# Two head slots per attention step, their products alternating between halves of the TensorE array

## The chip, the cores and the metric

The kernel runs on one core of one Trainium2 chip. The metric is device time in microseconds of one execution. Engines are named as the profile names them: PE is TensorE (its matmuls), PEld the weight loads of TensorE, DVE is VectorE, ACT is ScalarE, POOL is GpSimd, SP is SyncE, which issues the DMAs.

## The reference

Two layers, each a mixer of three branches and a SwiGLU feed-forward, over 256 positions of width 2048, in float32. The change touches the third branch, attention with 12 heads of 64 channels in 3 groups of 4 with (window, dilation) of (128, 1), (512, 4) and (2048, 16):

```python
scores = jnp.einsum("bhrnqd,bhrnkd->bhrnqk", qb, kb) * (HEAD_DIM ** -0.5)
dist = (dilation * np.abs(rel)).astype(np.float32)
bias = -slopes[:, None, None] * dist[None]
scores = jnp.where(valid, scores + bias[:, None, None], NEG)
lse = jax.nn.logsumexp(scores, axis=-1)
p = jnp.exp(scores - lse[..., None])
out = jnp.einsum("bhrnqk,bhrnkd->bhrnqd", p.astype(v.dtype), vb)
...
w = jax.nn.softmax(jnp.stack(lses, axis=0), axis=0)
o = jnp.sum(w[..., None] * jnp.stack(outs, axis=0), axis=0)
```

The three groups of one head slot (slot s has the heads s, 4+s and 8+s) are so combined that one softmax over the keys of all three groups gives the slot's output.

## The kernel before

All weights stream from HBM, 512 KB at a time. ACT copies each piece to a rounded form (`wh`), DVE subtracts to get the rest (`wl`), and PE multiplies both with the activations, which are kept with channels in the partitions. One step of such a product is a 512-column matmul with `wh` and a 256-column matmul with `wl`; a piece of 1024 columns has eight steps. `piece()` asks for loads and splits some pieces ahead.

Work that is not a weight product is put into the queue `beside`, as pairs of a function and a cost. `product` calls `some(0.9)` after each piece, which pops entries until their costs add up to 0.9; `drain()` pops all that is left, and is called before the first `branch`. So the attention's parts are written between pieces of the products that run meanwhile: the gates in layer 0, the short convolution's `zb` and the gates in layer 1. A scheduler then sets each engine's final order. On PE it can move an instruction ahead into a place where it reckons PE would wait.

Attention works on units (s, b): slot s of 4, and half b of the positions as queries. The positions are kept in such an order that the keys of groups 1 and 2 lie in the same half as the query. So a unit's score tile has 512 columns: 256 keys of group 0, 128 of group 1, 128 of group 2. There are 8 units in each layer. A unit has four parts:

- `att_scores` (L518): three float32 products into a PSUM tile `sc`; the 64 channels of a head are the upper or the lower 64 partitions (`po`) of the `q` and `kk` tiles. Then on DVE the bias (L531, three instructions), the maximum (L533) and its negative (L534).
- `att_soft`: exponential with its sum on ACT (L538), reciprocal and scaling on DVE (L539, L540).
- `att_turn`: four 128x128 transposes on PE (L545), one copy on ACT (L547).
- `att_out`: four float32 products with `v` (L554) into 64 of the partitions of a PSUM tile `o`, then a rounded copy on ACT (L559) and the rest on DVE (L560), into `csp`, which the branch products `yc` read.

`sc`, `pt` and `o` take turns in the three PSUM buffers of `aux`. The parts of one unit are popped 1 or 2 rounds apart (`lag`):

```python
units = [(s, b, {}) for s in range(HPG) for b in range(2)]
steps = [(att_out, 4, 0.4), (att_turn, 3, 0.0), (att_soft, 1, 0.6), (att_scores, 0, 1.5)]
```

Of the kernel before, what the change touches and what calls it, by code (L numbers as in the profile page):

```python
# [9 lines left out]
F32 = mybir.dt.float32  # L10
F32R = mybir.dt.float32r
I32 = mybir.dt.int32
AF = mybir.ActivationFunctionType
OP = mybir.AluOpType
AX = mybir.AxisListType

P = 128
S = 256
# [8 lines left out]
DH = 64  # L27
NG = 3
HPG = NH // NG
# [7 lines left out]
SLOPES = [2.0 ** (-8.0 * i / NH) for i in range(1, NH + 1)]  # L37
# [12 lines left out]
def trunk(ctx, tc, xt, win, wv, wy, wo, wgu, wd, cst, fin, dist, out):  # L50
    nc = tc.nc
# [5 lines left out]
    rp = ctx.enter_context(tc.tile_pool(name="rp", bufs=2))  # L57
# [7 lines left out]
    def tile2(name):  # L65
        return t2.tile([P, 2 * S], F32, tag="t2", name=name)

    def tile2r(name):
        return t2.tile([P, 2 * S], F32R, tag="t2", name=name)
# [20 lines left out]
    def acc(name):  # L90
        return pa.tile([P, 2 * S], F32, tag="acc", name=name)

    def aux(name):
        return px.tile([P, 512], F32, tag="aux", name=name)
# [4 lines left out]
    for l in range(DEPTH):  # L99
# [8 lines left out]
        for j in range(KD):  # L108
            for i in range(NGATE):
                n = N_ZA + N_QK + N_ZB + j * NGATE + i  # L110
# [47 lines left out]
    beside = deque()  # L158
# [22 lines left out]
    def product(dst, xs, whole=False, budget=0.9):  # L181


        k = 0
        while k < len(xs):
            wh, wl, nk = piece()
            for i in range(nk):
                c = slice(i * P, (i + 1) * P)
                x = xs[k]
                last = k == len(xs) - 1  # L190
                if whole:
                    nc.tensor.matmul(dst[:, :S], wh[:, c], turned(x[:, :S]), start=k == 0, stop=False)
                    nc.tensor.matmul(dst[:, :S], wh[:, c], turned(x[:, S:]), start=False, stop=False)
                else:
                    nc.tensor.matmul(dst, wh[:, c], turned(x), start=k == 0, stop=False)  # L195
                nc.tensor.matmul(dst[:, :S], wl[:, c], turned(x[:, :S]), start=False, stop=last)  # L196
                k += 1
            some(budget)
        return dst
# [57 lines left out]
    ident = cp.tile([P, P], F32, name="ident")  # L257
# [136 lines left out]
    for l in range(DEPTH):  # L394
# [14 lines left out]
        for i in range(2 * NCT):  # L409
            if l == 0 and i < 2:  # L410
# [5 lines left out]
                ps = two[i]  # L416
            else:
                ps = product(acc("za"), norm.operand(i))
# [62 lines left out]
        q, kk = [], []  # L481
# [7 lines left out]
        for i in range(N_QK):  # L489
            dst = kk if i >= N_QK // 2 else q  # L490
            n = 2 * NCT + i
            ps = product(acc("qk"), norm.operand(n))
# [4 lines left out]
        for g in range(NG):  # L497
            pv = [acc("v")[:, :S] for _ in range(2)]
            k = 0
            while k < KD:  # L500
                wh, wl, nk = piece()
                for i in range(nk // 2):
                    w = slice(i * S, (i + 1) * S)
                    for b in range(2):
                        hi = h[k][:, b * P:(b + 1) * P]
                        lo = h[k][:, S + b * P:S + (b + 1) * P]
# [7 lines left out]
                nc.scalar.copy(v[g][b], pv[b])  # L514


        csp = [None] * 2

        def att_scores(s, b, st):
            ps = aux("sc")  # L520
            sc = st["sc"] = tile2("sc")
            po = (s % 2) * DH
            for g in range(NG):
                t = (g * HPG + s) // 2
                a, n = (0, S) if g == 0 else (S + (g - 1) * P, P)
                keys = slice(0, S) if g == 0 else slice(b * P, (b + 1) * P)
                nc.tensor.matmul(ps[:, a:a + n], q[t][po:po + DH, b * P:(b + 1) * P], kk[t][po:po + DH, keys], start=True, stop=True)
            for g in range(NG):
                a, n = (0, S) if g == 0 else (S + (g - 1) * P, P)
                d = dsb[:, b * S:(b + 1) * S] if g == 0 else dsb[:, 2 * S + (g - 1) * P:2 * S + g * P]  # L530
                nc.vector.scalar_tensor_tensor(sc[:, a:a + n], d, SLOPES[g * HPG + s], ps[:, a:a + n], op0=OP.mult, op1=OP.add)  # L531
            m = st["m"] = rp.tile([P, 4], F32, tag="m", bufs=3, name="m")
            nc.vector.reduce_max(m[:, 0:1], sc, axis=AX.X)  # L533
            nc.vector.tensor_scalar_mul(m[:, 1:2], m[:, 0:1], -1.0)  # L534

        def att_soft(s, b, st):
            sc, m = st["sc"], st["m"]
            nc.scalar.activation(sc, sc, AF.Exp, bias=m[:, 1:2], accum_out=m[:, 2:3])  # L538
            nc.vector.reciprocal(m[:, 3:4], m[:, 2:3])  # L539
            nc.vector.tensor_scalar_mul(sc, sc, m[:, 3:4])  # L540

        def att_turn(s, b, st):
            pt_ps = aux("pt")
            for i in range(4):
                nc.tensor.transpose(pt_ps[:, i * P:(i + 1) * P], st["sc"][:, i * P:(i + 1) * P], ident)  # L545
            st["pt"] = tile2("pt")
            nc.scalar.copy(st["pt"], pt_ps)  # L547

        def att_out(s, b, st):
            po = (s % 2) * DH  # L550
            o = aux("o")[po:po + DH, :P]
            vs = [v[0][0], v[0][1], v[1][b], v[2][b]]
            for i in range(4):
                nc.tensor.matmul(o, vs[i][:, s * DH:(s + 1) * DH], st["pt"][:, i * P:(i + 1) * P], start=i == 0, stop=i == 3)  # L554
            if csp[s // 2] is None:
                csp[s // 2] = tile2r("csp")
            hi = csp[s // 2][po:po + DH, b * P:(b + 1) * P]
            lo = csp[s // 2][po:po + DH, S + b * P:S + (b + 1) * P]
            nc.scalar.copy(hi, o)  # L559
            nc.vector.tensor_sub(lo, o, hi.bitcast(F32))  # L560

        units = [(s, b, {}) for s in range(HPG) for b in range(2)]
        steps = [(att_out, 4, 0.4), (att_turn, 3, 0.0), (att_soft, 1, 0.6), (att_scores, 0, 1.5)]
        for n in range(len(units) + 4):
            for f, lag, cost in steps:
                u = n - lag
                if 0 <= u < len(units):
                    beside.append((lambda f=f, u=units[u]: f(*u), cost))
            beside.append((rest, 0.9))


        bsp = [None] * NCT
# [14 lines left out]
        gates, m = {}, []  # L587
# [34 lines left out]
        for j in range(KD):  # L622
            gs = []
            for i in range(NGATE):
                whole = j == KD - 1
                ps = product(acc("gate"), h, whole)
# [6 lines left out]
                n = BRANCHES.get(j * NGATE + i)  # L633
# [7 lines left out]
        for k in range(KD):  # L641
            ps = product(acc("wo"), m)
# [7 lines left out]
        for s in range(NSEG):  # L650
            f, gu = [], []
# [14 lines left out]
            for n in range(2 * FPS):  # L666
                ps = product(acc("fgu"), norm.operand(s * 2 * FPS + n), n == 2 * FPS - 1)
# [5 lines left out]
            for k in range(KD):  # L673
                whole = last and s == NSEG - 1 and k >= KD - 2
                ps = product(acc("fd"), f, whole)
# [109 lines left out]
```

## Time and profile before

| what | value |
|---|---|
| median of 3 runs | 2645.53 us (2645.19 to 2647.09) |
| the profiled execution | 2646.27 us, span 2644.5 us |
| PE busy | 2627.1 us, 99% of the span |
| DVE busy | 1901.2 us, 72% |
| ACT busy | 1455.4 us, 55% |
| DMA | 519.36 MB, mean 196 GB/s |
| granted clock over the span | 0.998 |

PE is busy nearly all the time, DVE and ACT have room, the weights arrive at less than the rate that the start of the trace shows. Matmuls are pipelined: the duration of one overlaps the next, so what a matmul costs is read from the distance of starts, not from its duration.

### The profile page before, as it was taken

The numbers are of one execution on the slowest core, as the hardware profiler recorded it, in microseconds if no ns is written. First come the engines' busy times: TensorE is split into PE (matmuls) and PEld (weight loads), VectorE is DVE, ScalarE is ACT, GpSimd is POOL, SyncE is SP. The second block draws the span as 40 slices with busy tenths as digits, with TensorE's granted clock in tenths as the row PEclk, the third lists the DMA queues.
The fourth block names the chain that finished last, engine by engine and source line by source line (L and its number), as shares of the span: only waits on it lengthen the run. The fifth ranks groups of instructions, "written<-read, shape, count | busy, mean of one in ns | idle before, by whom it ended". The sixth has DMA issues, their size and how long they took to land.

```text
span 2644.5 us, 42907 instructions
## 1 busy us (share of the span) xinstructions
PE 2627.1 (99%) x16744; PEld 2424.0 (92%) x16744; DVE 1901.2 (72%) x2924; ACT 1455.4 (55%) x2078; POOL 128.9 (5%) x93
## 2 busy tenths in 40 slices
PE   9999999999999999999999999999999999999998
PEld 8998899999999999999999989999999999999997
DVE  7997566678876666666899965666787666666665
ACT  6548655556645545445664575555565454454555
POOL 2000000011000000000102300000200000000002
PEclk9999999999999999999999999999999999999999
DMA  6665466666666656656566545665666566666664
GB/s 220 200 203 176 156 195 207 196 203 199 199 202 200 203 200 200 203 201 202 193 202 201 188 157 181 199 207 194 204 196 211 192 201 202 201 201 201 200 205 153
DMA packets 136749, 519.36 MB, mean 196 GB/s; under 512 B 15312, under 2 KB 17248, under 8 KB 136544
## 3 DMA queue, kind: packets, MB, share of 16 engines
q1 hardware_dynamic: 135648, 515.28, 59.3%
q8 instruction: 131, 2.15, 0.3%
q10 hardware_dynamic: 864, 1.31, 0.1%
q14 instruction: 74, 0.61, 0.1%
q0 software_dynamic: 32, 0.01, 0.0%
HBM read 514.45 MB, written 2.10 MB: 195 GB/s over the span
## 4 chain that ended last, share of the span: by engine, by line
PE 98%; DMA 0%; ACT 0%; issue 0%; POOL 0%; DVE 0%; SPq 0%; POOLq 0%; ACTq 0%
PE fgu L195 22%; PE gate L195 12%; PE fgu L196 12%; PE fd L195 11%; PE gate L196 6%; PE fd L196 6%; PE wo L195 4%; PE zb L195 3%; PE qk L195 3%; PE wo L196 2%; PE za L195 2%; PE zb L196 2%; PE qk L196 2%; PE yab L605 1%; PE yab L606 1%; PE yab L604 1%
## 5 line engine op out<-in xcount | busy, mean ns | idle before, releaser
L151 DVE TENSOR_TENSOR wl<-raw,wh 128x1024 fp32r<-128x1024 f32 (+3 forms) x1086 | 1217.0, 1121 | 616.3 <-ACT wh L150 606.2
L150 ACT CAST wh<-raw 128x1024 fp32r<-128x1024 f32 (+3 forms) x1086 | 1042.3, 961 | 1083.0 <-PE fgu L195 296.7
L195 PE MATMUL fgu<-xs,wh 128*128 128x512 f32 x2688 | 881.1, 382 | 0.0
L196 PE MATMUL fgu<-xs,wl 128*128 128x256 f32 x2816 | 768.2, 273 | 0.0
L195 PEld LDWEIGHTS fgu<-xs,wh 128*128 128x128 f32 x2688 | 508.0, 189 | 70.6
L196 PEld LDWEIGHTS fgu<-xs,wl 128*128 128x128 f32 x2816 | 540.7, 192 | 0.0
L195 PE MATMUL gate<-xs,wh 128*128 128x512 f32 x1440 | 477.2, 384 | 0.0
L195 PE MATMUL fd<-fs,wh 128*128 128x512 f32 x1386 | 454.4, 382 | 0.0
L196 PE MATMUL gate<-xs,wl 128*128 128x256 f32 x1536 | 419.3, 273 | 0.0
L196 PE MATMUL fd<-fs,wl 128*128 128x256 f32 x1408 | 383.8, 273 | 0.0
L195 PEld LDWEIGHTS gate<-xs,wh 128*128 128x128 f32 x1440 | 272.2, 189 | 38.0
L195 PEld LDWEIGHTS fd<-fs,wh 128*128 128x128 f32 x1386 | 262.0, 189 | 36.4
L196 PEld LDWEIGHTS gate<-xs,wl 128*128 128x128 f32 x1536 | 294.9, 192 | 0.3 <-issue 0.3
L196 PEld LDWEIGHTS fd<-fs,wl 128*128 128x128 f32 x1408 | 270.3, 192 | 0.0
L298 POOL TENSOR_TENSOR sq<-sq 128x256 f32<-128x256 f32 x59 | 63.7, 1079 | 2189.8 <-ACT sq L293 2189.8
L195 PE MATMUL wo<-mj,wh 128*128 128x512 f32 x512 | 167.6, 382 | 0.0
L196 PE MATMUL wo<-mj,wl 128*128 128x256 f32 x512 | 138.9, 273 | 0.0
L195 PE MATMUL zb<-xs,wh 128*128 128x512 f32 x384 | 127.0, 384 | 0.0
L195 PE MATMUL qk<-xs,wh 128*128 128x512 f32 x384 | 126.0, 382 | 0.2 <-ACT wh L150 0.2
L195 PEld LDWEIGHTS wo<-mj,wh 128*128 128x128 f32 x512 | 96.5, 189 | 13.3
L196 PE MATMUL zb<-xs,wl 128*128 128x256 f32 x384 | 105.0, 274 | 0.0
L196 PE MATMUL qk<-xs,wl 128*128 128x256 f32 x384 | 104.4, 273 | 0.0
(174 smaller groups left out, 3055.4 us busy)
## 6 DMA issues: line engine op xcount, KB each, us to landing
raw<-in_wgu SPq DMA_DIRECT2D x352, 512.0 KB, 4.2
raw<-in_win SPq DMA_DIRECT2D x318, 512.0 KB, 3.6
raw<-in_wd SPq DMA_DIRECT2D x128, 704.0 KB, 4.0
raw<-in_wo SPq DMA_DIRECT2D x64, 512.0 KB, 4.2
raw<-in_wy SPq DMA_DIRECT2D x32, 640.0 KB, 4.6
raw<-in_wv SPq DMA_DIRECT2D x24, 512.0 KB, 3.9
x<-in_xt SPq DMA_DIRECT2D x7, 256.0 KB, 6.8
out_y<-x ACTq DMA_DIRECT2D x4, 256.0 KB, 3.3
```

The costliest lines, as they stand in the source:

```text
L150: nc.scalar.copy(wh[:, :b - a], raws[ci][:, a:b])
L151: nc.vector.tensor_sub(wl[:, :b - a], raws[ci][:, a:b], wh[:, :b - a].bitcast(F32))
L195: nc.tensor.matmul(dst, wh[:, c], turned(x), start=k == 0, stop=False)
L196: nc.tensor.matmul(dst[:, :S], wl[:, c], turned(x[:, :S]), start=False, stop=last)
L298: nc.gpsimd.tensor_add(self.sums[0], self.sums[0], sq)
L604: nc.tensor.matmul(dsts[k], wh[:, w], turned(ys[k][:, :S]), start=k in first, stop=False)
L605: nc.tensor.matmul(dsts[k], wh[:, w], turned(ys[k][:, S:]), start=False, stop=False)
L606: nc.tensor.matmul(dsts[k], wl[:, w], turned(ys[k][:, :S]), start=False, stop=k in final)
```

## The change

The unit becomes (t, b): a pair of slots 2t and 2t+1, which lie in the upper and the lower 64 partitions of the same `q` and `kk` tiles. There are 4 such units in a layer in place of 8. The products of the two slots are written in turn: scores alternate between the upper and the lower 64 rows of the array (into two PSUM tiles), outputs between its two halves of 64 columns (into the two halves of one PSUM tile). The negated maximum, the reciprocal and the copies to `csp` are done once for both slots. The entries of `beside` all have cost 1, so one part is popped after each piece.

```diff
-        def att_scores(s, b, st):
-            ps = aux("sc")
-            sc = st["sc"] = tile2("sc")
-            po = (s % 2) * DH
+        def att_scores(t, b, st):
+            st["ps"] = [aux("sc") for _ in range(2)]
+            st["sc"] = [tile2("sc") for _ in range(2)]
+            st["m"] = rp.tile([P, 8], F32, tag="m", bufs=3, name="m")
             for g in range(NG):
-                t = (g * HPG + s) // 2
                 a, n = (0, S) if g == 0 else (S + (g - 1) * P, P)
                 keys = slice(0, S) if g == 0 else slice(b * P, (b + 1) * P)
-                nc.tensor.matmul(ps[:, a:a + n], q[t][po:po + DH, b * P:(b + 1) * P], kk[t][po:po + DH, keys], start=True, stop=True)
+                for i, ps in enumerate(st["ps"]):
+                    po = slice(i * DH, (i + 1) * DH)
+                    nc.tensor.matmul(ps[:, a:a + n], q[g * 2 + t][po, b * P:(b + 1) * P], kk[g * 2 + t][po, keys], start=True, stop=True)
+
+        def att_far(t, b, st, i):
+            sc, ps = st["sc"][i], st["ps"][i]
             for g in range(NG):
...
+            nc.vector.reduce_max(st["m"][:, i:i + 1], sc, axis=AX.X)
+
+        def att_soft(t, b, st):
+            m = st["m"]
+            nc.vector.tensor_scalar_mul(m[:, 2:4], m[:, 0:2], -1.0)
+            for i, sc in enumerate(st["sc"]):
+                nc.scalar.activation(sc, sc, AF.Exp, bias=m[:, 2 + i:3 + i], accum_out=m[:, 4 + i:5 + i])
+
+        def att_share(t, b, st):
+            m = st["m"]
+            nc.vector.reciprocal(m[:, 6:8], m[:, 4:6])
+            for i, sc in enumerate(st["sc"]):
+                nc.vector.tensor_scalar_mul(sc, sc, m[:, 6 + i:7 + i])
...
+        def att_out(t, b, st):
+            o = aux("o")[:, :P]
             vs = [v[0][0], v[0][1], v[1][b], v[2][b]]
             for i in range(4):
-                nc.tensor.matmul(o, vs[i][:, s * DH:(s + 1) * DH], st["pt"][:, i * P:(i + 1) * P], start=i == 0, stop=i == 3)
...
+                for n in range(2):
+                    s = 2 * t + n
+                    nc.tensor.matmul(o[n * DH:(n + 1) * DH], vs[i][:, s * DH:(s + 1) * DH], st["pt"][n][:, i * P:(i + 1) * P],
+                                     start=i == 0, stop=i == 3)
...
-        units = [(s, b, {}) for s in range(HPG) for b in range(2)]
-        steps = [(att_out, 4, 0.4), (att_turn, 3, 0.0), (att_soft, 1, 0.6), (att_scores, 0, 1.5)]
-        for n in range(len(units) + 4):
+        units = [(t, b, {}) for t in range(2) for b in range(2)]
+        steps = [(att_out, 2, ()), (att_turn, 1, (0,)), (att_scores, 0, ()), (att_turn, 1, (1,)), (att_far, 0, (0,)), (att_far, 0, (1,)),
+                 (att_soft, 0, ()), (att_share, 0, ())]
+        for n in range(len(units) + 2):
```

On PE, the first scores of layer 0, before (one slot, upper half of the rows; `gate` are the gate products that run meanwhile, `qk` the q and k tiles):

```order
L196 MATMUL gate_2530<-xs_983,wl_2534 128x256
L527 MATMUL sc_2587<-qk_1106,qk_746 128x256
L527 MATMUL sc_2587<-qk_1220,qk_868 128x128
L527 MATMUL sc_2587<-qk_1334,qk_990 128x128
L195 MATMUL gate_2603<-xs_528,wh_2567 128x512
```

The same place after (`sc_2587` is written from the upper 64 rows, `sc_2588` from the lower):

```order
L196 MATMUL gate_2530<-xs_983,wl_2534 128x256
L531 MATMUL sc_2587<-qk_1106,qk_746 128x256
L531 MATMUL sc_2588<-qk_1106,qk_746 128x256
L531 MATMUL sc_2587<-qk_1220,qk_868 128x128
L531 MATMUL sc_2588<-qk_1220,qk_868 128x128
L531 MATMUL sc_2587<-qk_1334,qk_990 128x128
L531 MATMUL sc_2588<-qk_1334,qk_990 128x128
L195 MATMUL gate_2603<-xs_528,wh_2567 128x512
```

Two bursts of three products, 32 rows of gate products apart, have become one burst of six. All 16 bursts of the two layers become 8 in this way, none is cut.

On PE, the first output products of a unit in layer 0, before:

```order
L196 MATMUL gate_2802<-xs_983,wl_2806 128x256
L554 MATMUL o_2847<-pt_2781,v_1527 64x128
L554 MATMUL o_2847<-pt_2781,v_1529 64x128
L554 MATMUL o_2847<-pt_2781,v_1667 64x128
L554 MATMUL o_2847<-pt_2781,v_1805 64x128
L545 MATMUL pt_2855<-ident_132,sc_2652 128x128 x4
```

After (`pt_2767` is the first slot's turned tile, `pt_2835` the second's; at the first "..." stand 48 rows of gate products, at the second 15):

```order
L567 MATMUL o_3001<-pt_2767,v_1527 64x128
L567 MATMUL o_3001<-pt_2835,v_1527 64x128
L567 MATMUL o_3001<-pt_2767,v_1529 64x128
...
L567 MATMUL o_3001<-pt_2835,v_1529 64x128
...
L567 MATMUL o_3001<-pt_2767,v_1667 64x128
L567 MATMUL o_3001<-pt_2835,v_1667 64x128
L567 MATMUL o_3001<-pt_2767,v_1805 64x128
L567 MATMUL o_3001<-pt_2835,v_1805 64x128
```

The scheduler has put some of the eight products into earlier places. Over both layers the eight units have their outputs in pieces of 3+1+4 (three units), 3+5 (two), 8 (one) and 1+7 (two): 18 bursts in place of 16.

On PE, the end of the last unit in layer 0, after (`yc` are branch products; before, the last output products stood 49 rows of gate products ahead of the first branch product; at the "..." stand 17 rows of gate products, 4 of them, the other six outputs and 12 rows of gates, and 10 rows of gates):

```order
L619 MATMUL yc_3495<-csp_3010,wh_3496 128x256
L556 MATMUL pt_3469<-ident_132,sc_3350 128x128 x4
L556 MATMUL pt_3476<-ident_132,sc_3351 128x128 x4
L620 MATMUL yc_3495<-csp_3010,wl_3497 128x256
...
L567 MATMUL o_3483<-pt_3474,v_1527 64x128
...
L567 MATMUL o_3483<-pt_3481,v_1527 64x128
...
L618 MATMUL yc_3495<-csp_3466,wh_3496 128x256
...
L619 MATMUL yc_3495<-csp_3466,wh_3496 128x256
```

The last unit's transposes and outputs now stand inside the first branch's products. Outside the attention's stretches no engine's order changes.

## Rows read from the trace of the kernel before

**Rows 1.** The page's chain of waits, shares of the span by engine.

```profile
PE 98%; DMA 0%; ACT 0%; issue 0%; POOL 0%; DVE 0%; SPq 0%; POOLq 0%; ACTq 0%
```

**Rows 2.** Windows: stretch, its length, busy of PE, PEld, DVE, ACT, POOL.

```profile
221.00:288.00 67.00, 67.00 (x408) 58.49 (x407) 46.29 (x92) 55.84 (x81) 0.00 (x0) 1.00 0.47 157
1513.00:1606.00 93.00, 93.00 (x573) 81.42 (x573) 60.86 (x117) 67.12 (x102) 0.00 (x0) 1.00 0.46 154
```

**Rows 3.** Groups by line and shape, whole run: count, busy us, mean ns.

```profile
L554 PE MATMUL o<-pt,v 128*64 128x128 f32 x128 | 17.4, 279 | 0.0
L527 PE MATMUL sc<-qk 64*128 64x256 f32 x32 | 11.1, 428 | 0.0
L545 PE MATMUL pt<-ident,sc 128*128 128x128 f32 x64 | 10.4, 285 | 0.0
L527 PE MATMUL sc<-qk 64*128 64x128 f32 x64 | 9.7, 271 | 0.0
```

**Rows 4.** PE timeline, first scores: start, length, count in a narrow window.

```profile
221.10 0.27 PE L196 MATMUL gate<-xs,wl 128*128 128x256 f32 x1
221.43 0.27 PE L196 MATMUL gate<-xs,wl 128*128 128x256 f32 x1
221.63 0.48 PE L527 MATMUL sc<-qk 64*128 64x256 f32 x1
221.96 0.60 PE L527 MATMUL sc<-qk 64*128 64x256 f32 x3
222.17 0.49 PE L527 MATMUL sc<-qk 64*128 64x128 f32 x3
222.71 0.48 PE L195 MATMUL gate<-xs,wh 128*128 128x512 f32 x1
223.03 0.27 PE L196 MATMUL gate<-xs,wl 128*128 128x256 f32 x1
```

**Rows 5.** PEld timeline, loads of those scores and of the first outputs.

```profile
221.63 0.18 PEld L527 LDWEIGHTS sc<-qk 64*128 64x128 f32 x1 [0.23 <-issue]
221.74 0.40 PEld L527 LDWEIGHTS sc<-qk 64*128 64x128 f32 x2
...
248.09 0.85 PEld L554 LDWEIGHTS o<-pt,v 128*64 128x64 f32 x8 [0.23 <-issue]
```

**Rows 6.** PE timeline, the first outputs and the transposes behind them.

```profile
247.89 0.27 PE L196 MATMUL gate<-xs,wl 128*128 128x256 f32 x1
248.09 1.09 PE L554 MATMUL o<-pt,v 128*64 128x128 f32 x8
249.11 0.66 PE L545 MATMUL pt<-ident,sc 128*128 128x128 f32 x4
249.52 0.46 PE L195 MATMUL gate<-xs,wh 128*128 128x512 f32 x1
249.82 0.27 PE L196 MATMUL gate<-xs,wl 128*128 128x256 f32 x1
```

**Rows 7.** DVE and ACT in layer 0: a timeline row, then groups by shape.

```profile
223.92 0.79 DVE L531 SCALAR_TENSOR_TENSOR sc<-dsb,sc 128x256 f32<-128x256 f32 x3
...
L151 DVE TENSOR_TENSOR wl<-raw,wh 128x1024 fp32r<-128x1024 f32 x19 | 23.2, 1221 | 6.5 <-ACT wh L150 6.5
L533 DVE TENSOR_REDUCE m<-sc 128x1 f32<-128x512 f32 x7 | 4.7, 678 | 0.1
L540 DVE TENSOR_SCALAR sc<-sc,m 128x512 f32<-128x512 f32 x7 | 3.4, 487 | 0.2
...
L150 ACT CAST wh<-raw 128x1024 fp32r<-128x1024 f32 x18 | 18.6, 1036 | 5.0 <-issue 4.9
L538 ACT ACT_TABLE_LOAD x7 | 9.0, 1283 | 0.1
L538 ACT ACTIVATE sc<-sc,m 128x512 f32<-128x512 f32 x7 | 5.1, 722 | 0.1
L547 ACT COPY pt<-pt 128x512 f32<-128x512 f32 x4 | 2.3, 584 | 0.0
```

More of the change, by code (lines that the diff above doesn't have):

```diff
@@ L530, in att_scores @@
                 d = dsb[:, b * S:(b + 1) * S] if g == 0 else dsb[:, 2 * S + (g - 1) * P:2 * S + g * P]
[L531 to L540, printed above, removed]
@@ L542, in att_turn @@
-        def att_turn(s, b, st):
+                nc.vector.scalar_tensor_tensor(sc[:, a:a + n], d, SLOPES[g * HPG + 2 * t + i], ps[:, a:a + n], op0=OP.mult, op1=OP.add)
+            nc.vector.reduce_max(st["m"][:, i:i + 1], sc, axis=AX.X)
[4 more added lines that the diff above has]
+                nc.scalar.activation(sc, sc, AF.Exp, bias=m[:, 2 + i:3 + i], accum_out=m[:, 4 + i:5 + i])
@@ L543, in att_turn @@
+        def att_share(t, b, st):
[3 more added lines that the diff above has]
+                nc.vector.tensor_scalar_mul(sc, sc, m[:, 6 + i:7 + i])
+        def att_turn(t, b, st, n):
             pt_ps = aux("pt")
             for i in range(4):
-                nc.tensor.transpose(pt_ps[:, i * P:(i + 1) * P], st["sc"][:, i * P:(i + 1) * P], ident)
-            st["pt"] = tile2("pt")
-            nc.scalar.copy(st["pt"], pt_ps)
@@ L549, in att_out @@
-        def att_out(s, b, st):
-            po = (s % 2) * DH
-            o = aux("o")[po:po + DH, :P]
+                nc.tensor.transpose(pt_ps[:, i * P:(i + 1) * P], st["sc"][n][:, i * P:(i + 1) * P], ident)
+            pt = tile2("pt")
+            st.setdefault("pt", []).append(pt)
+            nc.scalar.copy(pt, pt_ps)
+        def att_out(t, b, st):
+            o = aux("o")[:, :P]
             vs = [v[0][0], v[0][1], v[1][b], v[2][b]]
             for i in range(4):
-                nc.tensor.matmul(o, vs[i][:, s * DH:(s + 1) * DH], st["pt"][:, i * P:(i + 1) * P], start=i == 0, stop=i == 3)
[L555 to L558, printed above, removed]
+                for n in range(2):
+                    s = 2 * t + n
+                    nc.tensor.matmul(o[n * DH:(n + 1) * DH], vs[i][:, s * DH:(s + 1) * DH], st["pt"][n][:, i * P:(i + 1) * P],
+                                     start=i == 0, stop=i == 3)
+            if csp[t] is None:
+                csp[t] = tile2r("csp")
+            hi = csp[t][:, b * P:(b + 1) * P]
+            lo = csp[t][:, S + b * P:S + (b + 1) * P]
@@ L559, in att_out @@
             nc.scalar.copy(hi, o)
             nc.vector.tensor_sub(lo, o, hi.bitcast(F32))
-        units = [(s, b, {}) for s in range(HPG) for b in range(2)]
-        steps = [(att_out, 4, 0.4), (att_turn, 3, 0.0), (att_soft, 1, 0.6), (att_scores, 0, 1.5)]
-        for n in range(len(units) + 4):
[L565 to L569, printed above, removed]
+        units = [(t, b, {}) for t in range(2) for b in range(2)]
@@ L572, in trunk @@
+        steps = [(att_out, 2, ()), (att_turn, 1, (0,)), (att_scores, 0, ()), (att_turn, 1, (1,)), (att_far, 0, (0,)), (att_far, 0, (1,)),
+                 (att_soft, 0, ()), (att_share, 0, ())]
+        for n in range(len(units) + 2):
+            for f, lag, args in steps:
+                if 0 <= n - lag < len(units):
+                    beside.append((lambda f=f, u=units[n - lag], args=args: f(*u, *args), 1))
+            beside.append((rest, 1))
         bsp = [None] * NCT
```

## Prediction, made before the changed kernel ran

> **What bounds the kernel now.** I read the chain of waits first: PE makes up 98% of it [rows 1], so time is saved by taking work off PE, or lost by making PE wait. Then the windows over the two stretches in which attention runs, 221 to 288 us in layer 0 and 1513 to 1606 us in layer 1: PE is busy for the whole of both, 67.00 of 67.00 us and 93.00 of 93.00, at a granted clock of 1.00, with DVE busy for 46 and 61 us and ACT for 56 and 67 [rows 2]. So in these stretches only the pace of PE's stream counts. What a product costs there is the distance of starts in the timeline; the mean durations of [rows 3] (271 to 428 ns) overlap, and I use only the counts: 96 records for 48 score products, 128 for 64 output products, so a float32 product is two passes; the 64 transposes have one record each.
>
> **The price of a burst.** Between two `wl` matmuls of the gates there are 0.33 us when nothing stands between (221.10 to 221.43) and 1.60 us with a burst of scores (221.43 to 223.03) [rows 4]. The burst costs 1.27 us. Its passes have a pitch of 0.21 to 0.22 us for 256 columns (221.96 to 222.17) and 0.11 us for 128 (three passes take 0.49 us, the last one 0.27 of it) [rows 4]: 2 x 0.216 + 4 x 0.11 = 0.87 us. The other 0.40 us is the change of the array's shape from 128 rows to 64 and back, 0.20 us at each end. One sees it as a first pass that starts 0.20 us behind the `wl` matmul, where 0.11 would do, and whose successor comes after 0.32 us in place of 0.22, since the first weight load waits until then: PEld shows 0.23 us without work ahead of it [rows 5].
>
> For outputs: 247.89 to 249.82 is 1.93 us with an output burst and four transposes in it [rows 6], so 1.60 us for both. Transposes: 4 x 0.11 = 0.44. Output passes: 8 x 0.109 = 0.87. That leaves 0.29 us for the two changes of shape (64 columns and back). An output burst costs 1.16 us.
>
> Attention on PE before: 16 x (1.27 + 1.16 + 0.44) = 45.9 us, 1.7% of the time.
>
> **The change part by part.**
>
> Scores. 16 bursts become 8, so eight pairs of shape changes go: 8 x 0.40 = 3.2 us, whatever else happens. The 12 passes of a burst now alternate in pairs between upper and lower rows. No place of the trace has products of the two halves next to each other, so their price is bounded from the nearest rows. Upper bound without a price for alternating: one after another, 4 x 0.216 + 8 x 0.11 = 1.74 us. Lower bound: both halves wholly at once, 0.87. Between: the two passes of one product follow each other, so only the second pass of one product can lie beside the first of the next. Stepping through the order gives 1.08 us. But there are also 12 weight loads of 128 columns, which follow each other at 0.11 us where nothing else holds them (221.63, 221.74 [rows 5]): 12 x 0.108 = 1.30 us. I take 1.30, the row nearest to what then limits. Saved: 8 x (2 x 1.27 - 0.40 - 1.30) = 6.7 us; one after another 3.2; wholly at once 10.1.
>
> Outputs. The scheduler cut the eight units into 18 bursts where there were 16, so shape changes cost 2 x 0.29 = 0.6 us more. Passes one after another: nothing saved, so -0.6 us. With the second pass beside the next first, a burst of n alternating products takes n + 1 steps of 0.109 us in place of 2n: 3+1+4 takes 11, 3+5 takes 10, 8 takes 9, 1+7 takes 10; over the three, two, one and two units 33 + 20 + 9 + 20 = 82 steps, 8.9 us in place of 128 x 0.109 = 13.95. Saved 5.0 - 0.6 = 4.4 us. The loads don't limit here: eight take 0.85 us beside eight passes of the same pace, with half the columns [rows 5]. Wholly at once would be 78 steps: 4.9 us.
>
> Transposes: still 64, at the same 0.11. Cutting them (3+1 in two units) costs nothing, since the step from transposes to gates shows no change of shape: four start at 249.11, the next `wl` at 249.82 [rows 6], 0.71 = 4 x 0.11 + 0.05 of the shape change + 0.22.
>
> DVE and ACT. The negated maximum, the reciprocal and both copies to `csp` are issued half as often, and the exponentials of two slots share a table load (1.28 us each [rows 7]; the program has 24 table loads in place of 36). All of it lies beside a full PE: worth 0. The new lumps are also hidden: the bias and maximum of two slots, 2 x (0.79 + 0.67) us [rows 7], fall on two pieces of 2.6 us (8 x 0.33), with 1.22 us of `wl` work on each. That is 5.4 us of about 5.2, and the piece behind them has room.
>
> The PSUM buffers. Five `aux` tiles go through three buffers in a round. The second score tile takes the buffer of the last `o`, which DVE has to have read. 32 gate rows (5.2 us) or more stand between; in the trace ACT and DVE get there sooner, as PE's full windows show.
>
> The end of layer 0. The last unit's transposes now follow its scores by 48 gate rows (7.9 us), an output burst (1.2 or more) and 26 branch rows of 256 columns (2.8): 12 us. Until then DVE and ACT need 2 x 0.79 + 2 x 0.67 of bias and maximum, 1.28 table, 2 x 0.72 exponentials, 2 x 0.49 scaling [rows 7], and some 0.7 by my estimate for the signs, sums and reciprocals: 7.3 us, with one `wh` (1.04) and one or two `wl` (1.22 for 1024 columns) in between about 10. The outputs follow 17 gate rows (2.8 us) behind, for two copies (2 x 0.58) and one `wh`. So no long wait is due; if each is late by one such instruction, 2 us. I take 0.5.
>
> Sum: 6.7 + 4.4 - 0.5 = 10.6 us. Against the profiled execution, 2646.3 - 10.6 = 2635.7; that one is 0.7 above the median of the runs, so I say 2635.0.
>
> **A rule weighed against a row.** In the output bursts a weight load lies beside a pass that uses the same 128 rows: eight loads within 0.85 us, while the eight passes run without a gap [rows 5, 6]. The Trainium skill (TensorE: Matmul & The Clock Gate, Part 3, under "The mechanism") says that loads overlap with matmuls in flight only when the row group differs; taken literally, outputs, which differ in columns alone, would gain nothing. By the rule the change would be worth 6.7 - 0.6 - 0.5 = 5.6 us, by the row 10.6. The row shows the overlap already, so the rule stands as a rival with a small chance.
>
> **Rivals.**
>
> 1. Halves don't run beside each other: the change only saves shape changes. 3.2 - 0.6 - 0.5 = 2.1 us, 2643.4. For it: no row shows two halves at once, and a float32 pass already runs at half the column rate of the gates' passes (128 columns in 0.11 us, where the gates' 768 take 0.33 [rows 4]). Against it: the loads of a next pass are seen ahead of it, so PE doesn't finish one before it starts the other.
>
> 2. Only scores overlap: 5.6 us, 2639.9, by the step above. Or only outputs: 3.2 + 4.4 - 0.5 = 7.1 us, 2638.4, if two tiles of 64 rows wait for each other.
>
> 3. The other side: each change of half costs what a change of shape does. There are 40 changes of half in the scores (5 in each burst) and 46 in the outputs (burst length less one, over the 18 bursts). At 0.20 and 0.145 us: 8.0 + 6.7 = 14.7 us, nothing overlapped, less the 2.6 of shape changes saved: 12.1 us slower, 2657.6. It decides from 2.6 / 86 = 0.03 us for each change on. For it: that is what the rows show when PE goes to another part of the array. Against it: there the shape changes too. The Trainium skill (TensorEngine Tiling (Array Packing), Key Properties) says that a change of mode drains the array and one of tile doesn't; no row here has a change of tile alone.
>
> 4. A wait at the end of layer 0 beyond what I priced: 2 us, 2636.5. It changes no sign.
>
> **How the numbers follow.** Overlap in both, 0.50, is the forecast; its own range is 2630.5 (wholly at once: 10.1 + 4.9) to 2637.5 (2 us of waits and a little less overlap). Scores alone 0.10, outputs alone 0.08, no overlap 0.20, slower 0.10, something else 0.02. From 2630 to 2644 lie all but the slower case. 0.2% is 5.3 us, about what a measurement here can tell from no change. Faster by more than it, below 2640.2: the first case, outputs alone and half of scores alone, 0.64. Within it: no overlap and the rest, 0.25. Slower: 0.11.
>
> **What would show it.** The distance of the two gate `wl` matmuls around a burst of scores less 0.33 us: 1.7 if the loads limit, 1.3 if both halves run wholly at once, 2.1 if they take turns, over 2.5 if each change of half costs. Around the one output burst of 8: 1.27 with overlap, 2.04 without. PE's windows should stay full up to the first branch. The forecast is wrong if the starts inside a burst keep the old pitch, if PEld shows a gap at each change of half, or if PE waits on `wl` where the scheduler cut the bursts, which would mean that DVE's lumps are not hidden.

## The result, and the profile after

The changed kernel takes 2631.43 us (median of 4 runs, 2630.73 to 2632.50) against 2645.91 for the kernel before: 14.5 us less, a ratio of 0.9946 with the interval 0.9933 to 0.9958. The forecast was 2635.0 in a range of 2630 to 2644, and 10.6 us less. The profiled execution took 2631.35 us, its span 2629.6.

The page's first part, busy time and share of the span, and its chain by engine:

```profile
PE 2612.2 (99%) x16744; PEld 2411.6 (92%) x16744; DVE 1894.6 (72%) x2900; ACT 1437.9 (55%) x2058; POOL 124.5 (5%) x93
...
PE 98%; DVE 0%; ACT 0%; issue 0%; DMA 0%; SPq 0%; POOL 0%; POOLq 0%; ACTq 0%
```

PE has as many records as before (16744) and is still the whole chain; it lost 14.9 us of busy time, which is the result. The windows over the attention's stretches (length; PE, PEld, DVE, ACT, POOL busy; granted clock):

```profile
221.00:288.00 67.00, 67.00 (x434) 59.68 (x433) 44.40 (x76) 48.09 (x74) 0.00 (x0) 1.00 0.54 179
288.00:350.00 62.00, 62.00 (x436) 56.56 (x435) 39.31 (x65) 36.68 (x58) 0.00 (x0) 1.00 0.56 179
1500.00:1606.00 106.00, 106.00 (x686) 94.16 (x686) 70.58 (x122) 73.01 (x112) 0.00 (x0) 1.00 0.54 175
```

PE stays full, through the end of layer 0's attention and its first branch too (288 to 350 us). In 221 to 288 us it gets through 434 records where it had 408 [rows 2]. That count shows no overlap by itself: 360 of them are gates, where 308 were, and 74 are attention, where 100 were, since part of the attention now stands later. What runs side by side is read from the timeline. The first scores, which answer to [rows 4], in PE's timeline (the count is of what a narrow window touches; the fourth and fifth row are the same burst cut at 221.43 and 221.74):

```profile
220.88 0.27 PE L196 MATMUL gate<-xs,wl 128*128 128x256 f32 x1
221.21 0.27 PE L196 MATMUL gate<-xs,wl 128*128 128x256 f32 x1
221.41 1.15 PE L531 MATMUL sc<-qk 64*128 64x256 f32 x12
221.41 0.49 PE L531 MATMUL sc<-qk 64*128 64x256 f32 x2
221.41 0.70 PE L531 MATMUL sc<-qk 64*128 64x256 f32 x4
222.49 0.48 PE L195 MATMUL gate<-xs,wh 128*128 128x512 f32 x1
222.81 0.27 PE L196 MATMUL gate<-xs,wl 128*128 128x256 f32 x1
```

221.21 to 222.81 is 1.60 us, less 0.33: the burst costs 1.27 us, to the hundredth what a burst of half as many passes cost before. Two passes are there by 221.43 and take 0.49 us together, 0.01 more than one alone; four take 0.70, as two did before. So the passes of the two slots run in pairs. Their weight loads do too. The first two passes and the first two loads before, when they followed one another, then PEld after, the first load and the first two:

```profile
221.63 0.70 PE L527 MATMUL sc<-qk 64*128 64x256 f32 x2
221.63 0.29 PEld L527 LDWEIGHTS sc<-qk 64*128 64x128 f32 x2 [0.23 <-issue]
...
221.41 0.18 PEld L531 LDWEIGHTS sc<-qk 64*128 64x128 f32 x1 [0.22 <-issue]
221.41 0.19 PEld L531 LDWEIGHTS sc<-qk 64*128 64x128 f32 x2 [0.22 <-issue]
```

Two loads take 0.19 us in place of the 0.29 that two in turn took. Outputs, a burst of two passes, one of six and one of 14, each between two gate matmuls:

```profile
250.94 0.38 PE L195 MATMUL gate<-xs,wh 128*128 128x512 f32 x1
251.25 0.65 PE L567 MATMUL o<-pt,v 128*64 128x128 f32 x6
...
252.04 0.38 PE L195 MATMUL gate<-xs,wh 128*128 128x512 f32 x1
...
259.58 0.38 PE L195 MATMUL gate<-xs,wh 128*128 128x512 f32 x1
259.89 0.43 PE L567 MATMUL o<-pt,v 128*64 128x128 f32 x2
...
260.46 0.38 PE L195 MATMUL gate<-xs,wh 128*128 128x512 f32 x1
...
315.23 0.38 PE L195 MATMUL gate<-xs,wh 128*128 128x512 f32 x1
315.54 1.09 PE L567 MATMUL o<-pt,v 128*64 128x128 f32 x14
316.55 0.38 PE L196 MATMUL gate<-xs,wl 128*128 128x256 f32 x1
316.77 0.38 PE L195 MATMUL gate<-xs,wh 128*128 128x512 f32 x1
```

From one `wh` to the next, less 0.33: two passes cost 0.55 us, six 0.77, 14 cost 1.21. With 0.109 us for each pair and for each pass without a partner, two, four and eight steps, 0.33 to 0.34 us of each is the change of shape. The waits of PE from 100 us to nearly the end:

```profile
PE rows L339 <- DVE root L332: 2.3, 1, 2.3
PE ms L323 <- ACT sq L293: 0.8, 1, 0.8
```

Both are norms outside the attention. No wait has come into it, at the end of layer 0 neither.

The sum from these prices: scores 8 x 1.27 = 10.2 us where there were 20.3; outputs 5 bursts of two passes, 5 of six, 3 of eight (0.79), 2 of ten (1.00), 3 of 14 or 16 (1.22), 14.7 us where there were 18.6. That is 14.0 of the 14.5 us. 0.2 us of the rest stands ahead of the first scores already (their last `wl` starts at 221.21, before at 221.43 [rows 4]), outside the attention; its cause is open.

### The profile page after: what moved, and what is told of

It is laid out like the page before. It is cut to its first block, busy times and chain, and to the rows that moved or that the text cites. A ratio compares the mean times of both kernels' runs of the same rounds, so it can differ in the third digit from the quotient of the medians.

```text
span 2629.6 us, 42869 instructions
## 1 busy us (share of the span) xinstructions
PE 2612.2 (99%) x16744; PEld 2411.6 (92%) x16744; DVE 1894.6 (72%) x2900; ACT 1437.9 (55%) x2058; POOL 124.5 (5%) x93
## 4 chain that ended last, share of the span: by engine, by line
PE 98%; DVE 0%; ACT 0%; issue 0%; DMA 0%; SPq 0%; POOL 0%; POOLq 0%; ACTq 0%
PE fgu L195 22%; PE gate L195 12%; PE fgu L196 12%; PE fd L195 12%; PE gate L196 6%; PE fd L196 6%; PE wo L195 4%; PE qk L195 3%; PE zb L195 3%; PE wo L196 2%; PE za L195 2%; PE qk L196 2%; PE zb L196 1%; PE yab L619 1%; PE yab L618 1%; PE yab L620 1%
## 5 line engine op out<-in xcount | busy, mean ns | idle before, releaser
L431 DVE SCALAR_TENSOR_TENSOR ac<-apad,csb,ac 128x256 f32<-128x256 f32 x240 | 108.0, 525 | 0.0
```

The costliest lines, as they stand in the source:

```text
L431: nc.vector.scalar_tensor_tensor(ac[i], apad[:, i, k:k + S], c(C_CW + i * CK + k), ac[i], op0=OP.mult, op1=OP.add)
```

## Experiments

Theory 1, after the trace: passes in different halves of the array run at the same time, and what is saved is exactly the passes that find a partner and the shape changes that fall away. Ahead of the runs it also said that passes find a partner only where their products are neighbours in the order. Theory 2: PE finds the free half by itself, wherever the products stand in the burst, so that one burst in place of two is what counts. Theory 3: the gain is fewer shape changes and the lighter load of VectorE and ScalarE, with the starts inside a burst at the old pitch.

**The halves themselves (e6_same_rows).** Both slots' scores are taken from the upper 64 rows: the kernel computes the first slot's scores twice and leaves out the second's. Nothing else differs.

```diff
-                    po = slice(i * DH, (i + 1) * DH)
+                    po = slice(0, DH)
```

> The changed kernel with both slots' scores taken from the upper 64 rows (it computes the scores of the first slot twice and leaves out the second's); order, counts and bursts are the changed kernel's. If two halves that work at once are the gain, a score burst now costs 12 passes one after another, 1.74 + 0.40 = 2.14 us in place of 1.27: 8 x 0.87 = 7.0 us more, 2638.4. If the gain of the scores lies in one burst in place of two, or in the order, it stays at 2631.4.

Measured: 2638.69 us, ratio to the kernel before 0.9972 (0.9962 to 0.9983), 7.3 us more than the changed kernel. The burst in PE's timeline:

```profile
221.31 0.27 PE L196 MATMUL gate<-xs,wl 128*128 128x256 f32 x1
221.51 2.02 PE L531 MATMUL sc<-qk 64*128 64x256 f32 x12
223.46 0.48 PE L195 MATMUL gate<-xs,wh 128*128 128x512 f32 x1
223.78 0.27 PE L196 MATMUL gate<-xs,wl 128*128 128x256 f32 x1
```

2.47 - 0.33 = 2.14 us, as theory 1 has it: the 12 passes follow one another. The scores' passes that find a partner in the other half are worth 7 us; one burst in place of two saves only the rest.

**All but the pairs (e3_no_pairs).** Shared sign, reciprocal and table load stay, but `att_scores` and `att_out` do one slot at a time, each in an entry of its own.

```diff
...
-        steps = [(att_out, 2, ()), (att_turn, 1, (0,)), (att_scores, 0, ()), (att_turn, 1, (1,)), (att_far, 0, (0,)), (att_far, 0, (1,)),
+        steps = [(att_out, 2, (0,)), (att_turn, 1, (0,)), (att_out, 2, (1,)), (att_scores, 0, (0,)), (att_turn, 1, (1,)), (att_scores, 0, (1,)), (att_far, 0, (0,)), (att_far, 0, (1,)),
```

> The changed kernel with its units, shared sign, reciprocal and table loads, but the scores of the two slots in two bursts with a piece of gates between, and their outputs slot after slot, mostly in bursts of their own. Theories 1 and 2: PE's cost of attention is that of the kernel before, 2644 to 2646, since what was saved on VectorE and ScalarE lies beside a full PE. Theory 3 as far as it speaks of VectorE and ScalarE: clearly below 2644.

Measured: 2645.27 us, ratio 0.9997 (0.9988 to 1.0005). What was saved on DVE and ACT is worth nothing that can be measured, since PE doesn't wait for them. The run is not wholly without partners: in three of the eight units the scheduler put the outputs of both slots into one burst of 16 passes, 1.58 us long as in e2_outs_in_turn below, so even the 0.9 us by which its median lies below that of the kernel before (2646.18, measured beside it) can't be put down to the lighter load.

**Scores in turn (e1_scores_in_turn).** The three products of one slot, then the three of the other; outputs alternate.

```diff
-            for g in range(NG):
...
-                for i, ps in enumerate(st["ps"]):
+            for i, ps in enumerate(st["ps"]):
+                po = slice(i * DH, (i + 1) * DH)
+                for g in range(NG):
...
```

> The changed kernel with the six score products of a unit written slot after slot (three of the upper rows, then three of the lower) and the outputs still alternating. Theory 1 (two halves run at once only where their products are neighbours in the order): a burst of scores costs about 2.1 us in place of 1.27, at most one pass of it beside another; 8 bursts, so 6 to 7 us more, and some 0.8 for two bursts that the scheduler cuts: about 2639. Theory 2 (PE finds the free half by itself wherever the products stand in the burst, so one burst is what counts, not the alternation): bursts stay near 1.3 us, about 2632. Theory 3 (the gain is fewer shape changes and less work on VectorE and ScalarE): 2632 too, with starts inside the burst at the old pitch.

Measured: 2637.01 us, ratio 0.9966 (0.9954 to 0.9979), 5.6 us more than the changed kernel: between the theories, and nearer to the first. The burst, and within it the rows from the third and fourth starts on:

```profile
221.07 0.27 PE L196 MATMUL gate<-xs,wl 128*128 128x256 f32 x1
221.28 1.68 PE L531 MATMUL sc<-qk 64*128 64x256 f32 x12
221.28 0.70 PE L531 MATMUL sc<-qk 64*128 64x256 f32 x2
221.81 0.49 PE L531 MATMUL sc<-qk 64*128 64x128 f32 x3
221.82 0.49 PE L531 MATMUL sc<-qk 64*128 64x256 f32 x3
...
223.21 0.27 PE L196 MATMUL gate<-xs,wl 128*128 128x256 f32 x1
```

From one `wl` to the other are 2.14 us, so the burst costs 2.14 - 0.33 = 1.81 us; e6_same_rows, where all passes follow one another, has 2.14 after the subtraction. The first two passes, of 256 columns, are the first slot's first product; at 221.81 the first pass of its second product (128 columns) starts. The pass of 256 columns that starts at 221.82 can only be the other slot's first: it goes ahead of three passes of the first slot that stand before it in the program and haven't started. So PE does look for a pass of the free half, but not from the burst's start. That contradicts theory 1 where it asks for neighbours in the order, and theory 2 where it has PE look through the whole burst. Six such bursts at 0.54 us more and two units whose burst the scheduler cut make 5.3 us of the 5.6. A cut unit costs 1.04 us more: from the first start of the first burst to that of the cut unit's second piece are 21.63 us here, 20.05 to the same unit's burst in the changed kernel, and of the 1.58 us between them 0.54 is the first burst's.

**Outputs in turn (e2_outs_in_turn).** Four products of one slot, then four of the other.

```diff
-            for i in range(4):
-                for n in range(2):
-                    s = 2 * t + n
+            for n in range(2):
+                s = 2 * t + n
+                for i in range(4):
```

> The changed kernel with the eight output products of a unit written slot after slot, the scores still alternating. 17 output bursts in place of 18. Theory 1: no two passes beside each other, 128 x 0.109 + 17 x 0.345 = 19.8 us against the 14.7 that the 18 bursts of the changed kernel cost: 5.1 us more, 2636.5. Theories 2 and 3: no more than 0.4 us from 2631.4.

Measured: 2634.80 us, ratio 0.9957 (0.9943 to 0.9970), 3.4 us more than the changed kernel, where theory 1 had 5.1 and the others 0.4 at most. One of the two whole bursts of layer 0 (the third row is the same burst from 308.07 to a point just behind 308.29):

```profile
307.60 0.27 PE L196 MATMUL gate<-xs,wl 128*128 128x256 f32 x1
307.80 1.58 PE L567 MATMUL o<-pt,v 128*64 128x128 f32 x16
308.07 0.55 PE L567 MATMUL o<-pt,v 128*64 128x128 f32 x4
309.31 0.38 PE L618 MATMUL yab<-asp,wh 128*128 128x256 f32 x1
```

The burst takes 1.58 us in place of 1.09. Three passes of the first slot start at a pitch of 0.11 from 308.07 on, and a fourth start follows within 0.01 us of the third, at 308.29: the other slot's first. The first slot has started five passes then, and three stand waiting. It is the same number as in the scores, from another place in the burst: PE goes past three waiting passes. So part of the passes still find a partner, and the run loses less than theory 1 said. The bursts that the scheduler cut fit: where only two products of the first slot stand ahead of the other's, three passes wait from the start, and both halves start together, here within 0.02 us:

```profile
291.33 0.34 PE L567 MATMUL o<-pt,v 128*64 128x128 f32 x2
```

**Groups of two (e5_twos).** A test of that number, on the kernel with whole output bursts below.

```diff
-            for g in range(NG):
+            for g, i in ((0, 0), (1, 0), (0, 1), (1, 1), (2, 0), (2, 1)):
...
-                for i in range(4):
-                    for n in range(2):
+                for i, n in ((0, 0), (1, 0), (0, 1), (1, 1), (2, 0), (3, 0), (2, 1), (3, 1)):
...
```

> The kernel with whole output bursts, the products in groups of two of one slot, then two of the other (scores: two, two, one, one). Written slot after slot, the first product of the other slot started while three waiting passes stood ahead of it, not while more did. If PE looks past three waiting passes, the other half starts with the first pass here too: a score burst 1.27 us, outputs behind it 1.03, time within 1 us of 2627.5. If it needs the other half's product as the very next one, each burst of scores costs some 0.4 us more and each whole unit of outputs some 0.4 more: 6 us, 2633.

Measured: 2627.64 us, ratio 0.9932 (0.9918 to 0.9945), 0.2 us from that kernel with its products alternating one by one (e4_whole_outs, 2627.49). Its scores and outputs, and the start of the scores:

```profile
244.17 0.27 PE L196 MATMUL gate<-xs,wl 128*128 128x256 f32 x1
244.37 1.16 PE L532 MATMUL sc<-qk 64*128 64x256 f32 x12
244.37 0.49 PE L532 MATMUL sc<-qk 64*128 64x256 f32 x2
245.45 1.15 PE L569 MATMUL o<-pt,v 128*64 128x128 f32 x16
...
246.85 0.27 PE L196 MATMUL gate<-xs,wl 128*128 128x256 f32 x1
```

Both halves start together (two passes, 0.49 us) although three waiting passes stand between. The outputs lose half a step, 0.06 us in a whole burst, and the scheduler made nine output bursts where that kernel has ten. The products need not alternate one by one.

**Whole output bursts (e4_whole_outs).** Both transposes go ahead of the next scores, so that the output tile takes the PSUM buffer of the second transpose, and the outputs get a higher priority; 10 output bursts in place of 18.

```diff
-            for i in range(4):
-                for n in range(2):
...
+            with tc.high_priority(2 * SOONER):
+                for i in range(4):
+                    for n in range(2):
...
-        steps = [(att_out, 2, ()), (att_turn, 1, (0,)), (att_scores, 0, ()), (att_turn, 1, (1,)), (att_far, 0, (0,)), (att_far, 0, (1,)),
+        steps = [(att_out, 2, ()), (att_turn, 1, (0,)), (att_turn, 1, (1,)), (att_scores, 0, ()), (att_far, 0, (0,)), (att_far, 0, (1,)),
```

> The changed kernel with both transposes of a unit ahead of the next scores, so that the output tile takes the buffer of the second transpose and all its products become ready together, and with the output products at a higher priority: 10 output bursts in place of 18, six of them directly behind scores. Each burst not cut saves a shape change (0.345 us) and lets the rest run in pairs (1.22 us for a whole unit in place of 1.57 to 2.1), and scores next to outputs share a change of some 0.15 us: 14.7 us for outputs become about 9.5, so 5 us less, 2626.3. If the early places that the scheduler chose for the cut pieces had filled real waits of PE, nothing is gained: 2631, and PE would wait for wl.

Measured: 2627.49 us, ratio 0.9931 (0.9918 to 0.9943): 3.9 us less than the changed kernel, 18.7 less than the kernel before. A unit's outputs behind another's scores:

```profile
244.74 0.27 PE L196 MATMUL gate<-xs,wl 128*128 128x256 f32 x1
244.94 1.15 PE L531 MATMUL sc<-qk 64*128 64x256 f32 x12
246.02 1.09 PE L568 MATMUL o<-pt,v 128*64 128x128 f32 x16
247.04 0.48 PE L195 MATMUL gate<-xs,wh 128*128 128x512 f32 x1
247.36 0.27 PE L196 MATMUL gate<-xs,wl 128*128 128x256 f32 x1
```

Scores and outputs cost 2.62 - 0.33 = 2.29 us together, where a burst of each for itself costs 1.27 + 1.22. PE is busy for the whole of its stretches in this run too (67.00 of 67.00 us from 221 to 288). So the early places that the scheduler gave the cut pieces filled no wait. Which of the two edits it takes was not tested. With e5_twos, from which it can't be told apart, it is the best version measured here; in two units the scores are still cut, in two the outputs (1 + 7).

## Why the prediction was right

**The bound.** Right: only PE's stream counts. The windows are full before and after, and e3_no_pairs shows the other engines' saved work to be worth nothing.

**The time.** 14.5 us were saved where 10.6 were forecast, near the end of the prediction's own range that has both halves wholly at once (2630.5). Of the 3.9 us more, the scores gave 3.4 and the wait that didn't come 0.5, the outputs fell 0.5 short, and 0.5 is not accounted for.

**The scores: the mechanism right, the size too small.** The 3.2 us of shape changes came: e6_same_rows, whose scores have one burst but no partners, is still 7.0 us ahead of the kernel before, 3.9 of them from the outputs. The overlap was priced by the row of weight loads in turn, 12 x 0.108 = 1.30 us for the passes of a burst, and by the step that only the second pass of one product can lie beside the first of the next. Both failed: loads of two halves start together, and the other slot's first pass starts with the first slot's first. The passes of a burst take 0.87 us, the lower bound, and the scores gave 10.1 us in place of 6.7. The trace of before could not show that; its loads all went to one half within a burst.

**The outputs: nearly right, in part by luck.** 4.4 us were forecast, 3.9 came, by two errors of opposite sign. Pairs were perfect here too (78 steps in place of 82, 0.4 us better), but the shape change was taken as 0.29 us from a burst with transposes behind it; between gates it is 0.34 to 0.345, over 18 bursts 0.9 us worse. The cutting was seen ahead and priced; what it could still give back, 4 us, was shown by e4_whole_outs.

**Waits.** 0.5 us were put in for the end of layer 0; none came.

**The rivals.** That halves don't run beside each other fell with the first timeline. That only one kind of product overlaps fell too: the outputs share all 128 rows, and e2_outs_in_turn loses 3.4 us when they are written slot after slot. With it fell the rule that the prediction weighs against a row: outputs differ in columns alone, and 14 passes of two slots take 1.09 us, as eight of one slot did [rows 6]. That each change of half costs what a change of shape does: 86 such changes cost nothing visible, 12 passes take the time of six. On changes of shape and of half the Trainium skill (TensorEngine Tiling (Array Packing), Key Properties) says that a change of mode drains the array, and that tiles load and multiply independently of each other. The trace agrees: about 0.20 us at each end of a burst of scores, none between halves. The Trainium skill (TensorEngine Tiling (Array Packing), Theoretical Speedup) gives up to twice the speed where one dimension is at most 64. The scores reach it: 0.87 us in place of the 1.74 of e6_same_rows.

## What to carry to other kernels

Where a product fills only half of the array's rows or columns, look for a second one for the other half and put the two next to each other in PE's order, in one burst: the second is then free, and a burst costs its two changes of shape, here 0.34 to 0.40 us, only once. After the change, read the order that the scheduler made: products cut off from their partners, or into several bursts, give part of the gain back. It paid here because PE's stream is the bound, as full windows of PE show; no run here shows it where another engine bounds.

## What the runs showed of the hardware that was not expected

PE starts matmul passes out of the program's order: a pass for a free half of the array went ahead of three waiting passes of the other half, in the scores and in the outputs alike, and did not start while more stood ahead (e1_scores_in_turn, e2_outs_in_turn; with three from the start it went at once, e5_twos). All bursts of the first two runs fit three waiting passes. Whether that is a fixed number or what these weight loads and passes leave was not settled. Weight loads of two halves run at the same time as well: two within 0.19 us, where two for the same half took 0.29.
